# Decoder layer on one core: the MLP's sums kept times the mean square, products in another order, gate by halves of the tokens, last norm token-major

## Chip, cores and metric

One core of one Trainium2 chip runs one step of a decoder layer. The metric is the device time of that program in microseconds (us), the median of several runs.

## The reference, cut to what matters

```python
def rms_norm(x, gain):
    y = xf * lax.rsqrt(jnp.mean(xf * xf, axis=-1, keepdims=True) + EPS)
    return y * gain
...
    x = x + jnp.concatenate([o, sg], axis=-1) @ w_out
    x = x + jnp.square(jax.nn.relu(rms_norm(x, g_ff) @ w_up)) @ w_down
    x = x + (p @ w_ple) * jax.nn.sigmoid(rms_norm(x, g_ple) @ w_ple_gate)
...
y_prompt = rms_norm(hp, g_final)
```

x has 1024 prompt tokens and 8 sample tokens of width 1024, the MLP has width 4096, p has width 256; all is float32. The mixer ahead of these lines (a gated delta rule and a spatial gate) isn't touched. Call X1 the x after the mixer. The relu is squared, so the factor of its norm can be taken out of the product: the MLP's sum over the rows of w_down is divided by the mean square of X1 (plus EPS) for each token.

## The kernel before

Activations lie feature-major: 128 features on the partitions, tokens along the row. Tokens are split into halves N1 and N2 (nn = 0, 1) and each of these into two pieces t of 256 and 260 columns (the 8 sample tokens lie at the end of the second), features of the result into halves M1 and M2 (ab). Every matmul operand is split into a high and a low part of type fp32r (`form`, `split_raw`, `split_gain`), and each product is three matmuls.

The up stage and the down stage multiply 2 x 2 blocks by the seven-product scheme of Winograd (P1 to P7). The up stage (`up_stage`) writes the squared relu and its sums to DRAM (f_d). Beside it `up_rows` writes X1 to DRAM (x1_d), sums its squares on ScalarE and GpSimd, and writes the reciprocal of the mean square of each token to row_d. The down stage (`down`) runs four quarters j of the inner dimension; each has the seven products in the order of DSTEPS, each product four column groups p of 128, each group two pieces t of 12 matmuls. It reads the activations of a product (raw, one buffer), splits them (`split_raw`), makes the weights of the next products four groups ahead (`down_forms`, RING = 4; GpSimd adds blocks of w_down where the scheme wants sums), and VectorE or ScalarE adds the PSUM tile to that product's accumulator:

```python
if j == 0:
    S.copy(a, ps)
else:
    V.tensor_add(a, a, ps)
```

In the last quarter the accumulators are added to each other, `finish` multiplies the MLP's sum by rr (the broadcast reciprocal), adds old X1 read back from DRAM and sums its squares, and `gate_in` multiplies by g_ple and splits for the gate. Then the gate: `gate_units((0, 2))` does eight column groups for N1, `gate_units((1, 3))` for N2. `rows` makes 1/rms for all tokens, `row_put` and `row_get` send it over DRAM to a broadcast tile; gate results wait in four PSUM tiles until it is there. `p_in` transposes p. Each block is multiplied by rr, put through a sigmoid, multiplied by the embedding product (`emb`) and added to X. The last norm sums squares feature-major on ScalarE and GpSimd, and `y_out` transposes and scales.

TensorE's order is the order of the program text, in which `weave` steps side tasks (`spawn`) into the matmuls by a hand-written clock (ROW, FIN0, YT, PT). In the down stage SP's DMA queue is in program order too. The other queues are ordered by the scheduler by priority and expected times; `high_priority` marks evictions and weights.

## Time and profile before

| | us |
|---|---|
| median of 3 runs (lowest, highest) | 1451.28 (1448.44, 1456.3) |
| the profiled execution | 1451.69 |
| its span | 1450.0 |
| TensorE busy in the span | 1322.1 |
| VectorE, ScalarE, GpSimd busy | 892.5, 676.9, 709.6 |

A busy share is an average over stages. PE is TensorE, PEld its weight loads, DVE VectorE, ACT ScalarE, POOL GpSimd, SP the queue that issues the DMAs; L1382 is line 1382 of the kernel. The granted clock is the share of full speed (2.4 GHz) that TensorE had on average in a stretch; its two levels are 1.2 and 2.4 GHz.

### The profile page before, as it was taken

The numbers are of one execution on the slowest core, as the hardware profiler recorded it, in microseconds if no ns is written. First come the engines' busy times: TensorE is split into PE (matmuls) and PEld (weight loads), VectorE is DVE, ScalarE is ACT, GpSimd is POOL, SyncE is SP. The second block draws the span as 40 slices with busy tenths as digits, with TensorE's granted clock in tenths as the row PEclk, the third lists the DMA queues.
The fourth block names the chain that finished last, engine by engine and source line by source line (L and its number), as shares of the span: only waits on it lengthen the run. The fifth ranks groups of instructions, "written<-read, shape, count | busy, mean of one in ns | idle before, by whom it ended". The sixth has DMA issues, their size and how long they took to land.

```text
span 1450.0 us, 26432 instructions
## 1 busy us (share of the span) xinstructions
PE 1322.1 (91%) x10195; PEld 1292.2 (89%) x10195; DVE 892.5 (62%) x1719; ACT 676.9 (47%) x1427; POOL 709.6 (49%) x723
## 2 busy tenths in 40 slices
PE   6979978989999899799999999799999999538997
PEld 5979967989898899799999999799999999438997
DVE  7746655366937747554554444466777788984454
ACT  6665646422233226544554445465334333244553
POOL 5300988847416316666755565434232239763411
PEclk9999989999999999899999999999999999768999
DMA  7234525555437713245444553744352435121232
GB/s 245 81 90 136 153 66 163 154 159 151 125 84 208 221 56 126 79 150 161 133 141 131 160 162 111 275 163 174 107 187 90 176 125 180 47 71 47 86 105 74
DMA packets 209177, 193.99 MB, mean 134 GB/s; under 512 B 20928, under 2 KB 183947, under 8 KB 205460
## 3 DMA queue, kind: packets, MB, share of 16 engines
q1 hardware_dynamic: 209052, 192.31, 42.3%
q8 instruction: 80, 1.31, 0.4%
q14 instruction: 45, 0.37, 0.1%
HBM read 131.76 MB, written 60.62 MB: 133 GB/s over the span
## 4 chain that ended last, share of the span: by engine, by line
PE 68%; POOL 10%; DVE 10%; ACT 4%; DMA 3%; issue 3%; SPq 1%; DVEq 0%; POOLq 0%; ACTq 0%
PE A L1209 9%; PE D L1209 6%; PE d L1422 6%; PE d L1423 6%; PE d L1421 6%; PE g L209 5%; PE g L211 4%; PE g L210 4%; PE B L1209 3%; PE C L1209 3%; POOL xinv L644 3%; POOL it L643 3%; PE g L1613 2%; PE g L1615 2%; PE g L1614 2%
## 5 line engine op out<-in xcount | busy, mean ns | idle before, releaser
L1422 PE MATMUL d<-h,wlo 128*128 128x260 f32 (+1 forms) x896 | 258.9, 289 | 30.7 <-DVE wlo L153 30.7
L209 PE MATMUL g<-ra,whi 128*128 128x384 f32 (+3 forms) x800 | 274.4, 343 | 1.2 <-ACT ra L388 1.0
L1421 PE MATMUL d<-h,whi 128*128 128x260 f32 (+1 forms) x896 | 257.8, 288 | 5.9 <-ACT whi L150 5.9
L211 PE MATMUL g<-ra,whi 128*128 128x384 f32 (+3 forms) x800 | 257.6, 322 | 0.8 <-POOL ra L389 0.4
L1423 PE MATMUL d<-h,whi 128*128 128x260 f32 (+1 forms) x896 | 257.7, 288 | 0.0
L210 PE MATMUL g<-ra,wlo 128*128 128x384 f32 (+3 forms) x800 | 256.6, 321 | 0.0
L1422 PEld LDWEIGHTS d<-h,wlo 128*128 128x128 f32 x896 | 174.5, 195 | 33.1 <-DVE wlo L153 33.1
L1421 PEld LDWEIGHTS d<-h,whi 128*128 128x128 f32 x896 | 173.9, 194 | 6.5 <-ACT whi L150 6.5
L1423 PEld LDWEIGHTS d<-h,whi 128*128 128x128 f32 x896 | 174.2, 194 | 0.0
L209 PEld LDWEIGHTS g<-ra,whi 128*128 128x128 f32 x800 | 155.4, 194 | 3.4 <-ACT ra L388 1.4
L211 PEld LDWEIGHTS g<-ra,whi 128*128 128x128 f32 x800 | 155.0, 194 | 2.5 <-POOL ra L389 1.6
L210 PEld LDWEIGHTS g<-ra,wlo 128*128 128x128 f32 x800 | 155.8, 195 | 0.7 <-DVE wlo L153 0.3
L153 DVE TENSOR_TENSOR wlo<-st,whi 128x512 fp32r<-128x512 f32 x94 | 74.6, 794 | 46.5 <-ACT whi L150 45.1
L1339 DVE TENSOR_TENSOR h<-raw,h 128x1024 fp32r<-128x1024 f32 (+1 forms) x56 | 79.6, 1429 | 28.6 <-ACT h L1338 28.6
L153 DVE TENSOR_TENSOR wlo<-s,whi 128x512 fp32r<-128x512 f32 x64 | 50.5, 790 | 75.7 <-ACT whi L150 75.7
L1209 PE MATMUL A<-fb,whi 128*128 128x260 f32 (+1 forms) x512 | 97.0, 282 | 0.0
L643 POOL TENSOR_TENSOR it<-ainv,xinv 32x31 f32<-32x31 f32 (+15 forms) x124 | 75.0, 605 | 40.2 <-DMA ainv<-inv_d 30.8
L1236 ACT ACTIVATE q<-q 128x520 f32<-128x520 f32 (+1 forms) x128 | 78.4, 631 | 25.3 <-DVE q L1232 19.8
L644 POOL TENSOR_TENSOR xinv<-xinv,it 32x31 f32<-32x31 f32 (+15 forms) x124 | 80.9, 653 | 9.6
L150 ACT CAST whi<-st 128x512 fp32r<-128x512 f32 x96 | 58.9, 618 | 52.2 <-PE g L211 32.4
L1209 PEld LDWEIGHTS A<-fb,whi 128*128 128x128 f32 x512 | 80.9, 189 | 0.0
L1338 ACT CAST h<-raw 128x1024 fp32r<-128x1024 f32 (+1 forms) x56 | 58.8, 1057 | 33.5 <-PE d L1422 21.8
(441 smaller groups left out, 3550.1 us busy)
## 6 DMA issues: line engine op xcount, KB each, us to landing
raw<-f_d SPq DMA_DIRECT2D x28, 1032.0 KB
a<-in_w_down SPq DMA_DIRECT2D x16, 1024.0 KB
st<-in_w_in SPq DMA_DIRECT2D x24, 512.0 KB
ck<-ck_d SPq DMA_DIRECT2D x32, 320.0 KB
f_d<-tt SPq DMA_DIRECT2D x16, 520.0 KB
ra<-in_w_up SPq DMA_DIRECT2D x32, 256.0 KB
rb<-in_w_up SPq DMA_DIRECT2D x32, 256.0 KB
f_d<-tt SPq DMA_DIRECT2D x16, 512.0 KB
```

The costliest lines, as they stand in the source:

```text
L153: lo_eng.tensor_sub(dst_lo, src, f32(dst_hi))
L209: PE.matmul(ps[:, :w], lhsT=whi[k], rhs=xh, start=(k == 0), stop=False)
L210: PE.matmul(ps[:, :w], lhsT=wlo[k], rhs=xh, start=False, stop=False)
L211: PE.matmul(ps[:, :w], lhsT=whi[k], rhs=xl, start=False, stop=(k == nk - 1))
L643: G.tensor_mul(tv, a, x)
L644: G.tensor_sub(X[:, j + 1 :, :w], X[:, j + 1 :, :w], tv)
L1209: PE.matmul(ps, lhsT=a[:, k, :], rhs=x[:, c, k, :], start=(first and k == 0 and j == 0), stop=(k == 3 and j == 2), skip_group_check=True)
L1236: S.activation(v, v, func)
L1339: V.tensor_sub(lo[:, c], raw[:, c], f32(hi[:, c]))
L1421: PE.matmul(ps, lhsT=wh[:, k, :], rhs=xh[:, k, :], start=(k == 0), stop=False)
L1422: PE.matmul(ps, lhsT=wl[:, k, :], rhs=xh[:, k, :], start=False, stop=False)
L1423: PE.matmul(ps, lhsT=wh[:, k, :], rhs=xl[:, k, :], start=False, stop=(k == 3))
```

## The change

All sums of X1 are kept multiplied by the mean square of the token (mst). `up_rows` multiplies old X1 by it on GpSimd, takes N2's part from N1's for the features of M2, and writes that to x1_d. The down stage loads it into four accumulators before the first product, so that the products are added onto it; no accumulator is multiplied by rr or gets old X1 at the end. Norms that follow don't see a factor common to a token if EPS is multiplied by its square (ems); p is multiplied by mst instead. P1 is added to two accumulators (INTO), all evictions are VectorE's, and the order of the products is P1, P6, P7, P4, P2, P5, P3. N1's inputs of the gate are ready after P2; N2's are made inside the gate stage (`second_half`), with a mean square of its own. The last norm is token-major: `y_out` transposes a chunk of tokens, squares and sums it on ScalarE along the row, takes the root, and multiplies by it and g_final.

In the diff below "..." stands for what is left out; `placed` and `issue_after` set the place of an instruction in its queue behind a named one.

```diff
-DSTEPS = (("P1", 0), ("P5", 4), ("P6", 5), ("P7", 6), ("P4", 3), ("P2", 1), ("P3", 2))
+DSTEPS = (("P1", 0), ("P6", 5), ("P7", 6), ("P4", 3), ("P2", 1), ("P5", 4), ("P3", 2))
...
+    def tok_put(i, nn, tok):
+        ps = pss.tile([P, 512], F32, tag="B0" if pss is pu else "s2", name="msT")[:5, :P]
+        PE.transpose(ps, tok, ident)
+        row = tp.tile([5, P], F32, tag="row", bufs=1, name="row")
+        V.tensor_copy(row, ps)
+        SY.dma_start(row_d[i, nn], row)
+    def tok_get(i, nn, c, out):
+        SY.dma_start(out, row_d[i, nn].rearrange("a b -> (a b)")[c : c + out.shape[1]].partition_broadcast(P))
...
+        G.memset(mst, 1.0)
...
-        V.reciprocal(tok, tok)
-        yield ROW
-        row_put(tok, 1, pu.tile([P, 512], F32, tag="B0", name="msT")[:, :P])
+        V.tensor_mul(ems, mst, mst)
+        V.tensor_scalar_mul(ems, ems, EPS)
+        for nn in range(2):
+            yield ROW
+            tok_put(0, nn, mst[:, nn])
+        for t in range(2):
+            w = WT[t]
+            mb = tp.tile([P, 520], F32, tag=f"sq{t}", bufs=1, name="mb")[:, : 2 * w].rearrange("p (a b) -> p a b", a=2)
+            for nn in range(2):
+                tok_get(0, nn, TOFF[t], mb[:, nn])
+            for m in range(KD):
+                x = X1[m][:, 512 * t : 512 * t + 2 * w].rearrange("p (a b) -> p a b", a=2)
+                G.tensor_mul(x, x, mb)
+                if m >= 4:
+                    G.tensor_sub(x[:, 0], x[:, 0], x[:, 1])
+                SY.dma_start(x1_d[m, :, 512 * t : 512 * t + 2 * w].rearrange("p (a b) -> p a b", a=2), x)
+                yield 5.0
...
-    acc = {"P1": ACC[:, 0, 0], "P6": ACC[:, 0, 1], "P7": ACC[:, 1, 0], "P5": ACC[:, 1, 1]}
-    for name in ("P4", "P2", "P3"):
-        acc[name] = dac.tile([P, 4, 516], F32, name=f"acc_{name}")
+    C11, C12, P4, P7 = ACC[:, 0, 0], ACC[:, 0, 1], ACC[:, 1, 0], ACC[:, 1, 1]
+    P5, P3 = (dac.tile([P, 4, 516], F32, name=f"acc_p{i}") for i in (5, 3))
+    INTO = {"P1": (C12, C11), "P6": (C12,), "P7": (P7,), "P4": (P4,), "P2": (C11,), "P5": (P5,), "P3": (P3,)}
...
-    rr = xst.tile([P, 2, 516], F32, name="rr")
+    pt = xst.tile([P, NU, DPLE], F32, name="pt")
...
-            sums = dst.tile([P, 4, 4, P], F32, tag="s", name="sums")
+            s1 = dst.tile([P, 4, 4, P], F32, tag="s1", name="s1")
+            s2 = dst.tile([P, 4, 4, P], F32, tag="s2", name="s2")
             for name, _ in DSTEPS:
                 for p in range(4):
                     with tc.high_priority(PRI):
...
+                        if name == "P6":
+                            G.tensor_add(s1[:, p], a_of("A21", p), a_of("A22", p))
+                            G.tensor_sub(s2[:, p], s1[:, p], a_of("A11", p))
+                            f = s2[:, p]
+                        elif name == "P5":
+                            f = s1[:, p]
+                        elif name in ("P7", "P3"):
                             f = dst.tile([P, 4, P], F32, tag="t", name="sd")
...
-    def finish(ab, nn, p, xo):
+    def add_ss(ab, nn, p):
         a = ACC[:, ab, nn, p]
-        V.tensor_mul(a, a, rr[:, nn])
-        G.tensor_add(a, a, xo[:, p])
...
+        x1_old(C11, 0, 0)
         split_raw(0)
         load_raw(1)
         load_a(0, "A21")
         load_a(0, "A22")
+        x1_old(P7, 1, 1)
         load_a(0, "A12")
-        row_get(rr, 1)
+        x1_old(P4, 1, 0)
+        x1_old(P3, 0, 1)
+        SY.dma_start(pt, p_prompt[0, 0].rearrange("(c p) d -> p c d", p=P))
...
-                    to = {"P2": "P1", "P3": "P6"}.get(name, name) if end else name
-                    a = acc[to][:, p, TOFF[t] : TOFF[t] + w]
                     with tc.high_priority(PRI):
-                        if j == 0:
-                            S.copy(a, ps)
-                        else:
-                            V.tensor_add(a, a, ps)
+                        for to in INTO[name]:
+                            a = to[:, p, TOFF[t] : TOFF[t] + w]
+                            if j == 0 and (to is P5 or name == "P1" and to is C12):
+                                V.tensor_copy(a, ps)
+                            else:
+                                V.tensor_add(a, a, ps)
...
-                    if name == "P6":
-                        add(G, "P6", "P1")
-                        add(G, "P1", "P2")
-                    elif name == "P7":
-                        add(G, "P7", "P6")
-                        add(G, "P6", "P5")
-                        add(V, "P5", "P7")
-                        add(G, "P6", "P3")
+                        eng.tensor_add(x[:, p], x[:, p], y[:, p])
+                    if name == "P7":
+                        add(G, P7, C12)
                     elif name == "P4":
-                        add(V, "P7", "P4")
-                        finish(1, 1, p, xo[1, 1])
+                        add(V, P4, P7)
+                        gate_in(1, 0, p)
+                        add_ss(1, 0, p)
                     elif name == "P2":
-                        finish(1, 0, p, xo[1, 0])
-                        gate_in(1, 0, p)
-                    elif name == "P3":
-                        finish(0, 0, p, xo[0, 0])
                         gate_in(0, 0, p)
+                        add_ss(0, 0, p)
...
-            elif i == 3:
-                xo[1, 1] = x1_old("A11", 1, 1)
-                xo[1, 0] = x1_old("A21", 1, 0)
-            elif i == 4:
-                xo[0, 0] = x1_old("A22", 0, 0)
-            elif i == 5:
-                xo[0, 1] = x1_old("A11", 0, 1)
         for p in range(4):
-            finish(0, 1, p, xo[0, 1])
+            G.tensor_add(C12[:, p], C12[:, p], P5[:, p])
+            V.tensor_add(P7[:, p], P7[:, p], P5[:, p])
+            G.tensor_add(C12[:, p], C12[:, p], P3[:, p])
...
-    for p in range(4):
-        for ab in range(2):
-            gate_in(ab, 1, p)
...
+    pt8 = [ty.tile([TS // 2, DPLE], F32, name=f"pt8{nn}") for nn in range(2)]
+    for nn in range(2):
+        SY.dma_start(pt8[nn], p_sample[0, 4 * nn : 4 * nn + 4, 0, :])
+    SY.dma_start(gfb, g_final.partition_broadcast(P))
...
+        for nn in range(2):
+            for q0 in (0, 2, 4):
+                qs = (q0, q0 + 1) if q0 < 4 else (4,)
+                for q in qs:
+                    src = pt[:, q // 2 * 4 + 2 * nn + q % 2, :] if q < 4 else pt8[nn]
+                    G.tensor_scalar_mul(src, src, mst[: rows_of(q), nn, q : q + 1])
...
+            arrived("p", nn)
...
+    def rows(nn):
+        ps = pss.tile([P, 16], F32, tag="s2", name="ms")
+        tok = tp.tile([P, 5], F32, tag="tok", bufs=2, name="tok")
+        V.memset(tok, 1.0)
...
+            root(tok[:, :], "rp", False)
+        yield ROW
+        with tc.high_priority(2 * PRI):
+            tok_put(1, nn, tok)
+            tok_get(1, nn, 0, rr[:, nn])
+        arrived("r", nn)
+    def y_out(nn, q):
+        r = rows_of(q)
+        c = q // 2 * 4 + 2 * nn + q % 2
+        yo = ty.tile([P, D], F32, tag="yo", bufs=2, name="yo")
+        st = tp.tile([P, 2], F32, tag="st2", bufs=2, name="st2")
+        pa = []
+        for a in range(2):
+            ps = pss.tile([P, 512], F32, tag="s2", name="yT")
+            for j in range(4):
+                PE.transpose(ps[:r, j * P : j * P + P], ACC[:, a, nn, j, q * P : q * P + r], ident)
+            S.activation(yo[:r, :512], ps[:r], AF.Square, accum_out=st[:r, a : a + 1])
+            pa.append(ps)
+            yield YT
+        V.tensor_add(st[:r, 0:1], st[:r, 0:1], st[:r, 1:2])
+        V.scalar_tensor_tensor(st[:r, 0:1], in0=st[:r, 0:1], scalar=1.0 / D, in1=ems[:r, nn, q : q + 1], op0=ALU.mult, op1=ALU.add)
+        root(st[:r, 0:1], "ry", True)
+        y = y_prompt[0, c * P : (c + 1) * P, :] if q < 4 else y_sample[4 * nn : 4 * nn + 4, 0, :]
+        for a in range(2):
+            b = slice(512 * a, 512 * a + 512)
+            V.scalar_tensor_tensor(yo[:r, b], in0=pa[a][:r], scalar=st[:r, 0:1], in1=gfb[:r, b], op0=ALU.mult, op1=ALU.mult)
+            SY.dma_start(y[:, b], yo[:r, b])
...
-                (V if q7 else G).tensor_add(xv, xv, t)
-                if q7 and m == KD - 1:
-                    S.activation(q7[0][:, n // 2, :w], xv, AF.Square)
-                    V.tensor_scalar_mul(xv, xv, gfin[:, m : m + 1])
-                else:
-                    if m == 0:
-                        S.activation(blk(ss, n), xv, AF.Square)
-                    else:
-                        q = tp.tile([P, 260], F32, tag="q", name="q")[:, :w]
-                        S.activation(q, xv, AF.Square)
-                        G.tensor_add(blk(ss, n), blk(ss, n), q)
-                    S.activation(xv, xv, AF.Copy, scale=gfin[:, m : m + 1])
+                (V if last and m > 5 else G).tensor_add(xv, xv, t)
...
+    def second_half():
+        for p in range(4):
+            for ab in (1, 0):
+                gate_in(ab, 1, p)
+                add_ss(ab, 1, p)
+                yield 2.0
+        yield 4.0
+        yield from rows(1)
     def first_out():
-        tok = tok_stat(ss, first)
-        yield FIN
-        for c in first:
-            while c == first[-1] and not gated:
-                yield 0.5
-            yo = ty.tile([P, D], F32, tag="yo", bufs=2, name="yo")
-            for a in range(2):
-                y_out(c, a, yt(c, a, pss, "s2"), tok, yo)
-                yield YT
-    gated = []
+        for q in range(5):
+            yield from y_out(0, q)
...
+        spawn(rows(0))
+        spawn(p_in())
+        spawn(second_half(), 6.0)
+        weave(gate_units((0, 2), False))
         spawn(first_out(), FIN0)
+        weave(gate_units((1, 3), True))
         drain()
+        for q in range(5):
+            for _ in y_out(1, q):
+                pass
```

## Rows read from the trace of the kernel before

**Rows 1.** The page: the busy tenths of TensorE and the granted clock in 40 equal slices.

```profile
PE   6979978989999899799999999799999999538997
PEclk9999989999999999899999999999999999768999
```

**Rows 2.** Stretches of the span, us from its start: length, then busy time and number of instructions of PE, PEld, DVE, ACT and POOL, granted clock, DMA share and GB/s.

```profile
1000.00:1195.00 195.00, 195.00 (x1639) 195.00 (x1639) 151.23 (x234) 79.06 (x110) 59.73 (x40) 1.00 0.40 142
1195.00:1287.80 92.80, 65.58 (x453) 63.45 (x452) 86.65 (x96) 27.34 (x41) 77.14 (x48) 0.83 0.29 97
1287.80:1320.00 32.20, 12.47 (x70) 11.63 (x69) 17.48 (x39) 14.53 (x26) 15.74 (x10) 0.69 0.22 65
1320.00:1434.70 114.70, 114.70 (x964) 114.68 (x964) 57.24 (x132) 58.75 (x128) 32.75 (x42) 1.00 0.25 75
916.00:940.00 24.00, 14.61 (x100) 13.78 (x98) 11.16 (x10) 11.88 (x21) 12.41 (x10) 0.86 0.78 274
```

**Rows 3.** Who TensorE waited for from 1000 to 1320 us: us in total, times, the longest.

```profile
PE d L1422 <- DVE wlo L153: 26.9, 9, 8.1
PE pT L1540 <- DMA pt<-in_p_prompt: 15.5, 1, 15.5
PE ms L1129 <- POOL ss L1386: 4.2, 1, 4.2
```

**Rows 4.** Groups of instructions from 1195 to 1290 us, shapes kept apart: count, busy us, mean ns of one, then the idle time before them.

```profile
L1382 DVE TENSOR_TENSOR acc<-acc,rr 128x516 f32<-128x516 f32 x16 | 22.5, 1409 | 0.0
L1383 POOL TENSOR_TENSOR acc<-acc,a 128x516 f32<-128x516 f32 x15 | 23.7, 1577 | 8.8 <-DVE acc L1382 8.8
L1437 POOL TENSOR_TENSOR acc<-acc 128x516 f32<-128x516 f32 x12 | 21.1, 1764 | 10.3 <-DVE acc L1430 10.3
L1437 POOL TENSOR_TENSOR acc<-acc,acc_P 128x516 f32<-128x516 f32 x8 | 14.5, 1822 | 0.0
L167 DVE SCALAR_TENSOR_TENSOR xs<-acc,vec,xs 128x516 fp32r<-128x516 f32 x8 | 10.8, 1356 | 0.0
L153 DVE TENSOR_TENSOR wlo<-a,whi 128x512 fp32r<-128x512 f32 x8 | 11.0, 1388 | 0.0
L153 DVE TENSOR_TENSOR wlo<-sd,whi 128x512 fp32r<-128x512 f32 x8 | 7.9, 991 | 1.8 <-ACT whi L150 1.8
L1430 DVE TENSOR_TENSOR acc<-acc,d 128x256 f32<-128x256 f32 x15 | 6.2, 410 | 2.0 <-PE d L1423 2.0
L1339 DVE TENSOR_TENSOR h<-raw,h 128x1040 fp32r<-128x1040 f32 x3 | 5.6, 1854 | 0.0
```

**Rows 5.** The same view from 1000 to 1200 us.

```profile
L153 DVE TENSOR_TENSOR wlo<-a,whi 128x512 fp32r<-128x512 f32 x28 | 26.2, 938 | 3.1 <-ACT whi L150 3.0
L153 DVE TENSOR_TENSOR wlo<-sd,whi 128x512 fp32r<-128x512 f32 x19 | 16.0, 843 | 2.7 <-ACT whi L150 2.7
L1339 DVE TENSOR_TENSOR h<-raw,h 128x1040 fp32r<-128x1040 f32 x18 | 24.8, 1379 | 0.2 <-ACT h L1338 0.2
L1430 DVE TENSOR_TENSOR acc_P<-acc_P,d 128x256 f32<-128x256 f32 x24 | 10.0, 416 | 0.6
L1360 POOL TENSOR_TENSOR sums<-sums,a 128x512 f32<-128x512 f32 x12 | 15.6, 1298 | 38.5 <-DVE wlo L153 38.5
```

**Rows 6.** Instructions in order of time at the gate's start: start us, us, engine, line; in brackets the idle time before it and who ended it.

```profile
1315.63 0.36 DVE L1136 TENSOR_SCALAR tok<-ms 128x2 f32<-128x2 f32 x4 [2.16 <-PE ms L1129]
1328.98 0.42 DVE L1589 TENSOR_TENSOR t<-g,rr 128x256 f32<-128x256 f32 x1 [2.71 <-DMA rr<-row_d]
```

**Rows 7.** Up stage: two groups of GpSimd from 600 to 905 us, one stretch (columns as in rows 2), and the two stores of the statistics row, with first and last start.

```profile
L1267 POOL TENSOR_TENSOR ssu<-ssu,qu 128x520 f32<-128x520 f32 x7 | 10.2, 1455 | 1.4 <-ACT qu L1266 1.4
L1246 POOL TENSOR_TENSOR tt<-q,tt 128x256 f32<-128x256 f32 x15 | 17.3, 1156 | 0.2
700.00:800.00 100.00, 100.00 (x841) 99.93 (x840) 48.58 (x91) 50.53 (x96) 60.95 (x53) 1.00 0.45 141
L1153 SPq DMA_DIRECT2D row_d<-row x2: 298/309/320, 741.6 to 1322.5; - x2
```

**Rows 8.** Start of the down stage: SP's DMA queue in order of time, and the stretch with the highest DMA rate (columns as in rows 2).

```profile
925.08 0.45 SPq L1331 DMA_DIRECT2D raw<-f_d  x1
925.58 2.51 SPq L1346 DMA_DIRECT2D a<-in_w_down  x3
934.89 34.16 SPq L1331 DMA_DIRECT2D raw<-f_d  x4
930.00:940.00 10.00, 7.96 (x65) 7.54 (x63) 3.47 (x3) 5.25 (x10) 4.76 (x4) 1.00 1.04 382
```

**Rows 9.** The tail, in order of time, of TensorE, ScalarE, VectorE and SP's queue.

```profile
1434.65 2.78 PE L1571 MATMUL yT<-ident,acc 128*128 128x128 f32 x24
1436.41 1.28 ACT L261 ACT_TABLE_LOAD   x1
1439.65 0.21 ACT L261 ACTIVATE rpr<-tok 128x9 f32<-128x9 f32 x1 [1.95 <-DVE tok L1138]
1440.81 1.41 DVE L1580 TENSOR_SCALAR yo<-yT,tok 128x512 f32<-128x512 f32 x2
1441.52 5.75 SPq L1581 DMA_DIRECT2D out<-yo  x10
1444.36 0.69 ACT L1578 ACTIVATE yo<-yT,tok 128x512 f32<-128x512 f32 x1 [1.50 <-DMA out<-yo]
```

More of the change, by code (lines that the diff above doesn't have):

```diff
@@ L1115, in trunk_step_kernel @@
     psx.close()
-    def chunk(v, c):
-        return v[:, :, 512:516] if c == NU else v[:, c // 2 % 2, TOFF[c // 4] + c % 2 * P : TOFF[c // 4] + c % 2 * P + P]
-    def tok_sums(ps, ss, chunks, more=None):
-        for c in chunks:
-            r = P if c < NU else TS
-            v = chunk(ss, c)
-            if c == NU:
-                s8 = tp.tile([P, 2, 4], F32, tag="s8", bufs=1, name="s8")
-                V.tensor_copy(s8, v)
-                v = s8.rearrange("p a b -> p (a b)")
-            PE.matmul(ps[:r, c : c + 1], lhsT=v, rhs=ones[:, 0:1], start=True, stop=not more)
-            if more:
-                PE.matmul(ps[:r, c : c + 1], lhsT=more[c], rhs=ones[:, 0:1], start=False, stop=True)
@@ L1149, in row_put, with rows_of @@
[L1149 to L1160 removed]
+    def rows_of(q):
+        return P if q < 4 else TS // 2
@@ L1278, in up_rows @@
+            v = ss.rearrange("p (a b) -> p a b", a=2)
+            for nn in range(2):
+                for q in (2 * t, 2 * t + 1) + ((4,) if t else ()):
+                    c = q % 2 * P if q < 4 else 256
+                    r = rows_of(q)
+                    PE.matmul(ps[:r, 5 * nn + q : 5 * nn + q + 1], lhsT=v[:, nn, c : c + r], rhs=ones[:, 0:1], start=True, stop=True)
+            pv = ps[:, :10].rearrange("p (a b) -> p a b", a=2)
             with tc.high_priority(PRI):
-                tok_mean(tok, ps, range(4 * t, 4 * t + 4 + t))
+                V.tensor_scalar(mst[:, :, 2 * t : 2 * t + 2], pv[:, :, 2 * t : 2 * t + 2], 1.0 / D, EPS, op0=ALU.mult, op1=ALU.add)
+                if t:
+                    V.tensor_scalar(mst[: TS // 2, :, 4], pv[: TS // 2, :, 4], 1.0 / D, EPS, op0=ALU.mult, op1=ALU.add)
@@ L1584, in gate_units @@
+    def gate_units(blocks, last):
         for m in range(KD):
@@ L1635, in trunk_step_kernel, with arrived @@
-    first, second = (0, 1, 4, 5), (2, 3, 6, 7, NU)
-    def first_out():
-        tok = tok_stat(ss, first)
-        yield FIN
-        for c in first:
-            while c == first[-1] and not gated:
-                yield 0.5
-            yo = ty.tile([P, D], F32, tag="yo", bufs=2, name="yo")
-            for a in range(2):
-                y_out(c, a, yt(c, a, pss, "s2"), tok, yo)
-                yield YT
-    gated = []
+    held, there = [], set()
+    def arrived(what, nn):
+        there.add((what, nn))
+        if there >= {("p", nn), ("r", nn)}:
+            for n, ev in list(held):
+                if n % 2 == nn:
+                    held.remove((n, ev))
+                    ev()
@@ L1683 @@
+        drain()
+        for q in range(5):
+            for _ in y_out(1, q):
+                pass
 _INS = [
```

190 lines of the change are left out of this document (50 added, 140 removed).

## Prediction

> **What bounds the kernel now.** First the page: TensorE's row of busy tenths is at 9 through the second half and drops in one place only, to 5, 3 and 8 shortly before the end, where the granted clock drops too [rows 1]. So the question is what that hole is worth and who makes it. Second, the stretches [rows 2]. From 1000 to 1195 us TensorE never pauses: 195 us for 1639 matmuls, 0.119 us each, 11.4 us for one of the seven products (96 matmuls). I use this as the yardstick: the lost time of a stretch is its length less 0.119 us per matmul recorded there, which counts idle time and time at the lower clock together (0.83, 0.69 of full speed). End of the down stage, 1195 to 1287.8: 453 matmuls are 53.9 us, lost 38.9. Start of the gate, 1287.8 to 1320: 70 matmuls are 8.3 us, lost 23.9. Start of the down stage, 916 to 940: 100 matmuls are 11.9 us, lost 12.1. The gate from 1320 to 1434.7 loses nothing, and from there to 1450.0 remain 15.3 us of tail. Third, who is waited for [rows 3]: 26.9 us for the low halves of weights (wlo) that VectorE writes, 15.5 for the p tokens, 4.2 for the sum of squares. Fourth, what keeps VectorE there: it is busy 86.65 of the 92.8 us and GpSimd 77.14 [rows 2], and the groups [rows 4] name finish (the products with rr, and GpSimd's additions of old X1) and the additions between accumulators.
>
> **End of the down stage.** The change removes the 16 VectorE products with rr, 22.5 us, and from GpSimd the additions of old X1, 23.7 us recorded there [rows 4]. Of the additions between accumulators GpSimd did 20 (21.1 + 14.5 us); 12 stay, four of them for the very end. VectorE keeps 8, and the 8 gate_in products (10.8 us). So VectorE has at least 86.65 - 22.5 = 64.2 us if nothing becomes shorter: lost 64.2 - 53.9 = 10.3. But its operations were stretched there: wlo took 1.39 and 0.99 us [rows 4] against 0.94 and 0.84 in the calm stretch [rows 5], split_raw 1.85 against 1.38. GpSimd falls to about 77.1 - 23.7 - 8 x 1.8 = 39 us, so part of this stretching goes; with the calm durations for 19 wlo and 6 split_raw, and a like share off 16 additions and products (1.4 to about 1.0), VectorE falls by another 15 us, below TensorE's work. Bounds of the lost time: 1 us, and 20 us if the order of VectorE's queue keeps weights behind additions as now (half of today's loss). I take 10, near the first sum, because queue order survives. Gain 29 (19 to 38).
>
> **Start of the gate.** p_prompt is now loaded at the start of the down stage instead of after w_ple into the same two buffers, so the 15.5 us go; the gate's first half needs only the sums of token half 0, complete after P2, two products (23 us) before the end, so the 4.2 us and most of the low clock go. What is late next is rr: from the mean square (1315.63) to the first product with it (1328.98) passed 13.4 us [rows 6]. Four PSUM tiles of gate work cover 4 x 24 x 0.119 = 11.4 us of it, and the p transposes some 2 more. The first 10 scalings of p on GpSimd, up to 1.2 us each by the 256-wide row [rows 7], can run earlier, since p and mst are there; behind the last C12 additions they would cost up to 12. w_ple waits for P5's buffer and lands after the last product, about as late as rr. Lost 5 instead of 23.9, bounds 1 and 14: gain 19 (10 to 23).
>
> **Start of the down stage.** Added on SP's queue ahead of load_raw(2) are four loads of old X1 (eight transfers, 1 MB each load) and p (1 MB), less rr and the later x1_old loads. raw(1), A21 and A22 leave at 925.1 to 928.1 [rows 8]; behind them 5 MB more. At the highest rate of that stretch, 382 GB/s, the 8.3 MB from 925.1 on end at 946.8, and raw(2), issued at 934.89 today, lands at about 949.5; its split (1.4 us on VectorE after ScalarE's half) is ready at about 952, where the third product could start at about 951. The second product is now P6, with one more GpSimd sum ahead of its weights, at least 1.3 us [rows 5]. With a short fall of the clock: +5 (0 to 12). The queue also gets a new wait at its head: the first x1_old load waits for the last x1_d write, and behind it stand raw(1), A21, A22 and A12, for which TensorE waits; a write later than 925 would cost its delay one for one.
>
> **Accumulating.** Every product is now added on VectorE: P1 twice (32 evictions more) and 56 ScalarE copies of the first quarter moved there, 88 x 0.41 = 36 us of VectorE. Its load in the calm stretch is 151.23 of 195 us [rows 2], 8.9 us per product of 11.4; 8 more evictions in 7 products make 9.4. So TensorE hides it, at no price. Where the cover goes: P1 alone, 8.9 + 3.3 = 12.2 us, spilling 0.8 us into the next product, within the four forms prepared ahead. The evictions read PSUM and keep 0.41 us in the busy stretch as in the calm one [rows 4, 5].
>
> **Up stage.** up_rows adds on GpSimd 16 products of 520 columns and 8 subtractions of half that: 16 x 1.46 + 8 x 1.16 = 33 us [rows 7], spread over 80 us in which GpSimd is already busy 61% (49 us): 82 of 80, so these low-ranked products drift some us behind their places and the weight sums between them can, too. The statistics land at 741.6 today, so the last x1_d write comes at about 825, well before the 925 of its first reader. TensorE is at 100% there [rows 7]: +2 (0 to 12).
>
> **Gate.** Two ScalarE passes per block and a GpSimd sum go: hidden, since TensorE never pauses there [rows 2], so 0. New are five token chunks put out during its second half, each with Squares, a root on ScalarE and two buffers yo that come back only after the store. One chunk needs about 4.4 us (two Squares at the 0.69 of a copy of that width, 0.4 for two small sums, 1.2 from Sqrt to the end of the four small operations behind it, 1.4 for two products [rows 9]) and 2.8 us until its store has landed (issued 1441.52, next write at 1444.36); two buffers give 7.2 / 2 = 3.6 us a chunk, while the order written for TensorE brings one every 3.9 (two YT of 1.2, stretched by the embedding's matmuls, and 8 transposes at 0.11). So about even: +3 (0 to 20), the tables' changes included: Sqrt among Sigmoids makes up to 10 changes of 1.28 us [rows 9], on a ScalarE half busy.
>
> The Trainium skill (ScalarE: Activation LUTs, What ACT_TABLE_LOAD costs) counts 2.66 us for a change, a drain included, and asks to batch functions by set, which speaks against this part. The trace has 1.28 and no row for a drain. By the Trainium skill's figure the tail would be 1.4 us longer and the sum 1423.
>
> **Tail.** From the end of the last embedding matmul (1434.65): transposes 0.5, Squares 1.4, sums 0.4, change of tables 1.3, 1.2, products 1.4: first chunk written at 1440.9, landed at 1443.7; the third, in the same buffer, 4.4 + 2.8 later at 1450.9; the fifth at 1458.1, against 1450.0 now [rows 9]. Bounds +2 (buffers not binding) and +10: +8.
>
> **Sum.** -29 - 19 + 5 + 2 + 3 + 8 = -30. The profiled execution took 1451.69 us, 1.7 above its span and 0.4 above the median: 1451.7 - 30 = 1422.
>
> **Rivals.** (a) A new wait takes the place of p at the gate's start: scalings of p behind C12's additions, or w_ple behind P5's buffer. For it: GpSimd was the late one there; against: both can run earlier. The whole 19 us go: 1441. (b) The output of chunks binds the second half of the gate: each of five costs its whole chain of 4.4 + 2.8 + 1.3 less the 3.9 of its place, 4.6 x 5 = 23 instead of 3: 1442. (c) VectorE becomes the bound of the whole down stage. If P6's doubled sums keep GpSimd so busy that VectorE works at the durations of [rows 4] throughout, a product needs 64 x 0.41 / 7 = 3.8 for evictions, 2 x 1.85 for the split and 4 x 1.39 for the forms, together 13.1 us against 11.4: 1.7 x 28 = 48 us lost, in which the end's 10 are included: 1422 + 38 = 1460, and with the clock falling in the pauses about 1465, slower. It decides from about 12.5 us a product. Against it: 77% today and evictions that don't stretch. (d) Stretching goes with GpSimd's work, and the three new costs hide (-38 - 21 + 8): 1401.
>
> **Chances.** Forecast 0.55 (alone 1409 to 1434), (a) 0.17, (b) 0.08, (c) 0.10, (d) 0.10. The range goes from (d), 1400, to 1446, above (a) and (b). About 0.5% (7 us) can be told from no change: faster than 1444 takes the forecast, (d) and most of (a) and (b), 0.84; same 0.07; slower, (c), 0.09.
>
> **What would show it.** After: no hole in TensorE's tenths but a notch at the gate's start; wlo waits under 12 us after the third quarter; no wait for p; VectorE about 82% in the middle of the down stage; TensorE at 100% through the up stage; a tail above 20 us with stores as releasers. I am wrong if VectorE reaches 100% in P1 and P6, if old X1 or raw(2) holds TensorE by 10 us or more, or if transposes wait for PSUM tiles in the gate's second half.

## The result: slower by half a per cent, in other places than forecast

The changed kernel takes 1460.43 us in the median of 17 runs against 1451.28 for 17 of the kernel before: ratio 1.0055, 95% interval 1.0038 to 1.0073. The forecast was 1422. The profiled execution took 1462.3 us (span 1460.6; before 1451.69 and 1450.0).

The page after, TensorE's busy tenths and its granted clock, to be held against [rows 1]:

```profile
PE   6979977989998999899949999769999999959996
PEclk9999989999999999999979999989999999989997
```

The hole before the end (5, 3, 8) is down to one 5. But there is a new hole (4) in the middle of the up stage and a deeper one (7, 6) at the start of the down stage. The stretches of the changed kernel (columns as in [rows 2]):

```profile
937.10:1000.10 63.00, 41.46 (x287) 40.30 (x287) 37.31 (x54) 18.21 (x26) 33.54 (x27) 0.81 0.68 238
1000.10:1293.40 293.30, 290.76 (x2407) 289.08 (x2406) 239.71 (x391) 117.98 (x167) 106.78 (x69) 0.99 0.37 129
1293.40:1321.40 28.00, 13.56 (x98) 12.64 (x97) 21.96 (x43) 15.94 (x30) 15.71 (x12) 0.76 0.28 85
700.00:765.00 65.00, 45.00 (x339) 44.09 (x338) 33.16 (x38) 18.58 (x34) 47.99 (x44) 0.82 0.48 156
```

By the yardstick of the forecast (length less 0.119 us per matmul; the tail is taken at its whole length), with the stages cut at the last matmul of each in either trace:

| stretch | lost before | lost after | difference | forecast |
|---|---|---|---|---|
| up stage from 560 us | 15.1 | 35.2 | +20.1 | +2 |
| first 63 us of the down stage | 12.1 | 28.8 | +16.7 | +5 |
| rest of the down stage | 39.2 | 6.9 | -32.3 | -29 |
| first 28 us of the gate | 21.8 | 16.3 | -5.5 | -19 |
| rest of the gate | 2.1 | 4.1 | +2.0 | +3 |
| tail | 15.9 | 22.8 | +6.9 | +8 |

That adds up to +7.9; the spans differ by 10.6, so 2.7 us are left for what lies ahead of 560 us. Three lines came out as forecast and three did not. The first line hides two opposite parts. The first 140 us of its stretch, before and after (columns as in [rows 2]):

```profile
560.00:700.00 140.00, 129.32 (x1051) 128.15 (x1050) 76.15 (x127) 79.22 (x153) 94.37 (x90) 0.95 0.40 127
560.00:700.00 140.00, 134.11 (x1099) 132.91 (x1098) 80.28 (x127) 80.88 (x157) 102.68 (x97) 0.99 0.37 118
```

Up to 700 us the loss fell from 14.9 to 9.2 us, and from there to the end of the up stage it rose from 0.1 to 26.0. The forecast has no term for the gain. In the kernel before ScalarE starts four squares of X1 from 581.08 us on, ahead of the next casts of the up stage's operands (586.18), and TensorE waits 5.9 us for such casts; the changed kernel ties the squares behind the up stage's own work, the casts start at 583.64, and the longest wait is 1.8. No run tests this by itself. Who TensorE waits for after 560 us (columns as in [rows 3], whose 26.9, 15.5 and 4.2 us have gone or shrunk):

```profile
PE d L1416 <- ACT whi L150: 16.0, 3, 10.6
PE D L1184 <- DVE wlo L153: 14.6, 2, 13.6
PE msT L1124 <- DVE tok L254: 13.4, 2, 12.7
PE yT L1582 <- DVE yo L1592: 9.2, 6, 4.2
PE d L1417 <- DVE wlo L153: 7.8, 6, 3.1
PE D L1184 <- ACT whi L150: 6.0, 1, 6.0
```

The same trace in order of time (start, us, engine, line; idle time before and its end in brackets), three excerpts: the up stage, the start of the down stage, the gate's start.

```profile
726.10 16.80 POOL L1273 TENSOR_TENSOR x<-x,mb 128x512 f32<-128x512 f32 x13 [4.82 <-DMA mb<-row_d]
742.86 1.26 POOL L1154 TENSOR_TENSOR s<-rb,ra 128x512 f32<-128x512 f32 x1
744.08 3.75 POOL L1273 TENSOR_TENSOR x<-x,mb 128x520 f32<-128x520 f32 x3
744.15 0.62 ACT L150 CAST whi<-s 128x512 fp32r<-128x512 f32 x1 [7.74 <-POOL s L1154]
744.80 14.11 DVE L153 TENSOR_TENSOR wlo<-s,whi 128x512 fp32r<-128x512 f32 x1 [11.21 <-ACT whi L150]
...
756.95 1.41 POOL L1223 TENSOR_TENSOR tt<-q,tt 128x256 f32<-128x256 f32 x2
758.97 0.58 PE L1184 MATMUL D<-fa,wlo 128*128 128x256 f32 x1 [13.56 <-DVE wlo L153]
759.05 1.59 POOL L1160 TENSOR_TENSOR s<-rb,ra 128x512 f32<-128x512 f32 x1 [0.69 <-DVE wlo L153]
...
942.65 3.19 SPq L1227 DMA_DIRECT2D f_d<-tt  x2
948.48 0.91 SPq L1369 DMA_DIRECT2D acc<-x_d  x2
949.49 0.46 SPq L1325 DMA_DIRECT2D raw<-f_d  x1
961.91 4.91 POOL L1353 TENSOR_TENSOR s<-a,a 128x512 f32<-128x512 f32 x4 [1.42 <-DMA a<-in_w_down]
966.78 5.86 POOL L1354 TENSOR_TENSOR s<-s,a 128x512 f32<-128x512 f32 x4
967.74 16.36 SPq L1325 DMA_DIRECT2D raw<-f_d  x2
...
1299.01 0.21 DVE L1564 SCALAR_TENSOR_TENSOR tok<-ms,ems 128x4 f32<-128x4 f32 x2
1299.15 1.65 DVE L167 SCALAR_TENSOR_TENSOR xt<-acc,vec,xt 128x516 fp32r<-128x516 f32 x1
1302.20 1.23 DVE L252 SCALAR_TENSOR_TENSOR rpt<-rpi,tok 128x5 f32<-128x5 f32 x1
1303.35 1.41 DVE L167 SCALAR_TENSOR_TENSOR xt<-acc,vec,xt 128x516 fp32r<-128x516 f32 x2
1312.88 0.17 DVE L254 SCALAR_TENSOR_TENSOR tok<-rpt,rpi 128x5 f32<-128x5 f32 x1
1313.61 0.28 DVE L1126 COPY row<-msT 5x128 f32<-5x128 f32 x1 [0.56 <-PE msT L1124]
1318.11 0.42 DVE L1601 TENSOR_TENSOR t<-g,rr 128x256 f32<-128x256 f32 x1 [0.23 <-DMA rr<-row_d]
```

In each a queue that runs in order holds small urgent work behind large work that is not urgent. Up stage: GpSimd starts 13 products of X1 in a row, and the weight sum (L1154) that TensorE needs comes behind them. Start of the down stage: SP's queue puts the first load of old X1 ahead of the second raw block, and GpSimd does four additions before the first difference. Gate: the small operations of N1's root, most of them 0.2 us each, alternate on VectorE with N2's gate inputs, then with p's low halves and w_ple's splits, and last from 1299.0 to 1312.9. What follows tests each.

### The profile page after: what moved, and what is told of

Same layout as the page of the kernel before. It is cut to its first block, busy times and chain, and to the rows that moved or that the text cites. A ratio compares the mean times of both kernels' runs of the same rounds, so it can differ in the third digit from the quotient of the medians.

```text
span 1460.6 us, 26483 instructions
## 1 busy us (share of the span) xinstructions
PE 1324.1 (91%) x10183; PEld 1290.2 (88%) x10183; DVE 914.0 (63%) x1832; ACT 651.7 (45%) x1361; POOL 690.9 (47%) x720
## 4 chain that ended last, share of the span: by engine, by line
PE 38%; DVE 7%; POOL 3%; issue 2%; DMA 2%; ACT 1%; SPq 0%; DVEq 0%; POOLq 0%; ACTq 0%
PE d L1417 6%; PE d L1418 6%; PE d L1416 6%; PE A L1184 5%; PE D L1184 3%; DVE wlo L153 2%; PE B L1184 2%; PE g L1614 2%; PE g L1615 2%; PE g L1616 2%; PE C L1184 2%; POOL x L1273 1%; DVE h L1333 1%; DMA a<-in_w_down 1%; DVE yo L1592 0%
## 5 line engine op out<-in xcount | busy, mean ns | idle before, releaser
L1416 PEld LDWEIGHTS d<-h,whi 128*128 128x128 f32 x896 | 172.6, 193 | 16.8 <-ACT whi L150 16.7
L153 DVE TENSOR_TENSOR wlo<-s,whi 128x512 fp32r<-128x512 f32 x96 | 94.0, 980 | 94.9 <-ACT whi L150 94.5
L150 ACT CAST whi<-s 128x512 fp32r<-128x512 f32 x96 | 59.3, 618 | 105.1 <-PE D L1184 26.5
L643 POOL TENSOR_TENSOR it<-ainv,xinv 32x31 f32<-32x31 f32 (+15 forms) x124 | 74.9, 604 | 40.0 <-DMA ainv<-inv_d 30.6
L1425 DVE TENSOR_TENSOR acc<-acc,d 128x260 f32<-128x260 f32 (+1 forms) x184 | 72.4, 414 | 28.6 <-PE d L1418 25.9
```

Source lines behind the costliest of these rows:

```text
L150: S.copy(dst_hi, src)
L153: lo_eng.tensor_sub(dst_lo, src, f32(dst_hi))
L643: G.tensor_mul(tv, a, x)
L1416: PE.matmul(ps, lhsT=wh[:, k, :], rhs=xh[:, k, :], start=(k == 0), stop=False)
```

## Experiments

Ratios are to the kernel before; "against the changed kernel" is the difference of the two ratios (the other is 1.0055) times 1451 us. Differences of under some 5 us say little by themselves: in the profiled executions the first matmul of the up stage, ahead of which no edit changes anything, comes anywhere from 575.6 to 584.5 us, and the up stage with the block of products in it varies by 5 us (last section). There the losses of the stretches decide.

| kernel | median us | ratio [95%] | against the changed kernel, us |
|---|---|---|---|
| e1_spread | 1433.2 | 0.9862 [0.9839, 0.9885] | -28 |
| e2_stores_late | 1459.5 | 1.0051 [1.0032, 1.0070] | -1 |
| e3_late_loads | 1453.7 | 1.0010 [0.9991, 1.0029] | -7 |
| e4_late_loads_alt | 1443.7 | 0.9950 [0.9921, 0.9980] | -15 |
| e5_rows_first | 1460.4 | 1.0050 [1.0035, 1.0064] | -1 |
| e10_row_first | 1455.0 | 1.0033 [1.0011, 1.0054] | -3 |
| e6_tail | 1452.0 | 1.0007 [0.9989, 1.0025] | -7 |
| e8_act | 1457.0 | 1.0053 [1.0033, 1.0073] | 0 |
| e9_finish_back | 1481.6 | 1.0199 [1.0172, 1.0225] | +21 |
| e7_all | 1418.0 | 0.9753 [0.9734, 0.9772] | -44 |
| e11_all | 1418.2 | 0.9783 [0.9764, 0.9802] | -39 |
| e12_all | 1409.6 | 0.9718 [0.9692, 0.9745] | -49 |

**The up stage: GpSimd's queue or SP's.**

```diff
+                with tc.issue_after(placed["pool"]):
+                    G.tensor_mul(x, x, mb)
+                    if m >= 4:
+                        G.tensor_sub(x[:, 0], x[:, 0], x[:, 1])
```

> Edit: the changed kernel, with GpSimd's X1 products and differences (L1273, L1275) each tied behind the latest store of an up period (the placed instruction of GpSimd), so that they stand singly between the periods' own work instead of as one block of 17 us. In the changed kernel TensorE had 339 products in the 65 us from 700 to 765 (24.7 us short of 0.119 us each), against next to nothing lost there in the kernel before. Theory A (the block in GpSimd's in-order queue holds back the weight sums, these the roundings, these TensorE): the loss in the up stage falls from 35 us to between 10 and 14 us, the time from 1460 to 1435 to 1442 us, that is 0.99 to 0.994 of the kernel before. Rival B (the products' volume on GpSimd is what is too much, wherever they stand): the loss spreads but stays at 20 us or more, the time stays over 1452 us. Rival C (it is the stores of X1 in SP's queue that hold back the weight loads): this order also spreads the stores, so A and C are told apart by the next kernel, not by this one.

```diff
-                SY.dma_start(x1_d[m, :, 512 * t : 512 * t + 2 * w].rearrange("p (a b) -> p a b", a=2), x)
+                stores.append((x1_d[m, :, 512 * t : 512 * t + 2 * w].rearrange("p (a b) -> p a b", a=2), x))
                 yield 5.0
+        for dst, x in stores:
+            with tc.issue_after(placed["sp"]):
+                SY.dma_start(dst, x)
+            yield 2.5
```

> Edit: the changed kernel with the X1 products left as one block, but each of their stores issued on SP later, between the up periods, so that the up stage's weight loads no longer stand behind a row of eleven stores that took 18 us. Theory A (GpSimd's queue): the weight sums still stand behind the block, TensorE still goes nearly without work for over 15 us near 745 us, and the loss in the up stage stays at 28 us or more; time 1453 to 1463 us. Theory C (SP's queue): the loss falls to under 18 us and the time to 1435 to 1445 us. Between them (20 to 27 us) both queues hold a part.

With the same products spread, the up stage loses 12.6 us, less than the 15.1 before the change. The stretch of e1_spread:

```profile
700.00:765.00 65.00, 65.00 (x536) 64.94 (x536) 37.38 (x59) 31.70 (x60) 51.49 (x42) 0.98 0.55 176
```

TensorE never pauses, while GpSimd is busy 51.49 of the 65 us, more than in the changed kernel (47.99). From 700 us to the end of the up stage e1_spread loses 1.6 us, against 0.1 in the kernel before and 26.0 with the block; that it loses less in all (12.6) comes from the time ahead of 700 us (11.0 for 14.9). The same stretch of e2_stores_late, with the stores moved and the block left:

```profile
700.00:765.00 65.00, 52.05 (x379) 50.64 (x378) 23.14 (x44) 21.63 (x40) 49.99 (x45) 0.87 0.30 93
```

Its up stage loses 30.5 us, and those of the five kernels with block and stores as they were, and without the long operation of the last section, lose 30.4 to 31.9. So it is GpSimd's order (the time of e1_spread is even 2 us below the range of theory A); the volume of products costs some 1.5 us, and the stores nothing that can be told.

**The start of the down stage: two queues.**

```diff
-        x1_old(C11, 0, 0)
         split_raw(0)
         load_raw(1)
         load_a(0, "A21")
         load_a(0, "A22")
-        x1_old(P7, 1, 1)
-        load_a(0, "A12")
-        x1_old(P4, 1, 0)
-        x1_old(P3, 0, 1)
-        SY.dma_start(pt, p_prompt[0, 0].rearrange("(c p) d -> p c d", p=P))
+        x1_old(C11, 0, 0)
...
             load_raw(n + 2)
+            if n == 0:
+                x1_old(P7, 1, 1)
+            elif n == 1:
...
```

> Edit: the changed kernel with the loads of old X1 into the accumulators, and that of the prompt rows, moved on SP's queue behind the second load of raw f blocks and the first A21 and A22, one in each of the next periods. In the changed kernel the start of the down stage (first 63 us) lost 28.8 us against 12.1 before; the second raw load came 12.3 us after the end of the up stage, against 8.9. Theory A (SP's queue, held by the first accumulator load, delays raw and the weights): the loss falls to 16 to 22 us, time 1448 to 1455 us. Rival B (the weight sums on GpSimd, whose four additions come ahead of the first difference, end last): raw comes earlier, but the roundings of s2 begin where they did, the loss stays within 3 us of 28.8 and the time at 1457 to 1463 us.

In e4_late_loads_alt the sums alternate too:

```diff
+                            with tc.issue_after(placed["sum"]) if p else ExitStack():
+                                G.tensor_add(s1[:, p], a_of("A21", p), a_of("A22", p))
+                            placed["sum"] = G.tensor_sub(s2[:, p], s1[:, p], a_of("A11", p)).ins
```

> Edit: the kernel of the late accumulator loads, with the weight sums of the down stage in the order addition, difference, addition, difference on GpSimd instead of four additions and then four differences. Theory A (loads alone): no more than 2 us better than the kernel with the late loads alone. Theory B (the order of the sums): the first rounding of s2 begins some 4 us earlier, 4.91 us of additions being four of 1.23 us, so the loss at the start of the down stage falls by 4 to 8 us against the late loads alone. With both, the loss is 10 to 18 us and the time 1442 to 1450 us.

Lost in the first 63 us: 28.8 in the changed kernel, 24.0 with the late loads, 17.3 with both. SP's queue in e3_late_loads, then GpSimd in e4_late_loads_alt:

```profile
942.72 0.45 SPq L1325 DMA_DIRECT2D raw<-f_d  x1
952.92 0.33 SPq L1325 DMA_DIRECT2D raw<-f_d  x1
```

```profile
950.45 1.28 POOL L1354 TENSOR_TENSOR s<-a,a 128x512 f32<-128x512 f32 x1 [0.24 <-DMA a<-in_w_down]
951.81 1.27 POOL L1355 TENSOR_TENSOR s<-s,a 128x512 f32<-128x512 f32 x1
```

The up stage ends at 933.9 in the first of these traces, so raw(1) leaves 8.8 us after it instead of 12.4 (949.49 - 937.1), and raw(2) 19.0 instead of 30.6 (967.74 - 937.1). Behind raw(1) stand the blocks of w_down that GpSimd adds: its first addition starts 24.8 us after the up stage in the changed kernel (961.91) and 20.7 in e3_late_loads, as in the kernel before. The loads alone brought 4.8 us, less than the 7 to 13 expected: there the first difference still stood behind four additions. In the second trace it comes 1.4 us after the first addition. So each queue held a part, 4.8 and 6.7 us.

**The gate's start: three links of one chain.**

```diff
+                with tc.issue_after(placed["root"]):
+                    gate_in(ab, 1, p)
...
+                    with tc.issue_after(placed["root"]):
+                        V.tensor_sub(lo, ps[:, :w], f32(hi))
```

> Edit: the changed kernel with VectorE's gate inputs of N2 and low halves of p tied behind the last operation of the root of N1's mean square, so that the nine small dependent operations of that root stand together in VectorE's queue. In the changed kernel the root took 13.9 us on VectorE (1299.0 to 1312.9) against 3.1 before (1315.6 to 1318.7), and TensorE waited 12.7 us for it. Theory A (other operations between the small ones): the root takes 3 to 5 us, the first product with rr comes about 9 us sooner, the first 28 us of the gate lose 6 to 9 instead of 16.3, the time is 1450 to 1455 us. Rival B (the covers end there, and p, w_ple or N2's inputs are late next): the root is short but the stretch still loses 13 us or more, or the gate after it loses what was gained; time 1457 to 1464 us.

```profile
1298.05 1.02 DVE L248 TENSOR_SCALAR rpi<-tok 128x5 int32<-128x5 int32 x1
1300.91 0.17 DVE L254 SCALAR_TENSOR_TENSOR tok<-rpt,rpi 128x5 f32<-128x5 f32 x1
1300.99 5.78 DVE L167 SCALAR_TENSOR_TENSOR xt<-acc,vec,xt 128x516 fp32r<-128x516 f32 x7
1306.69 0.41 DVE L1529 TENSOR_TENSOR pp<-pT,pp 128x256 fp32r<-128x256 f32 x1
1307.16 0.38 PE L1125 MATMUL msT<-ident,tok 128*5 128x128 f32 x1 [7.88 <-DVE pp L1529]
1312.90 0.27 DVE L1127 COPY row<-msT 5x128 f32<-5x128 f32 x1
```

In these lines of e5_rows_first the root takes 3.0 us (1298.05 to 1301.08), yet the row is copied at 1312.90: p's transposes stand ahead of the root's on TensorE and wait for low halves of p, which now stand behind seven gate inputs. The first 28 us of the gate lose 14.7 us. The theory of the root alone fell; the rival held.

```diff
-        V.tensor_copy(row, ps)
+        placed["row"] = V.tensor_copy(row, ps).ins
...
+                with tc.issue_after(placed["row"]):
+                    gate_in(ab, 1, p)
```

> Edit: the changed kernel with VectorE's gate inputs of N2 tied behind the copy of N1's statistics row (L1126), so that neither the root nor the low halves of p nor that copy stands behind them. With the root alone first (root 2.9 us instead of 13.9), TensorE still reached the transposition of the root at 1307.2, because p's transposes stand ahead of it and their low halves on VectorE stood behind seven gate inputs of N2; the copy of the row followed at 1312.9, behind the splits of w_ple. Theory A (the whole chain root, low halves of p, copy of the row, and not the root alone, sets the gate's start through VectorE's queue): the row is copied some 6 to 9 us earlier, the first 28 us of the gate lose 7 to 11 us instead of 16.3, and the time is 1450 to 1455 us. Rival B (after the row the gate's start waits for something else, such as the splits of w_ple or p's products on GpSimd): the row is early, but the loss stays at 13 us or more, time 1457 to 1464 us.

```profile
1295.24 0.28 DVE L1127 COPY row<-msT 5x128 f32<-5x128 f32 x1 [0.47 <-PE msT L1125]
1301.69 0.27 PE L1524 MATMUL pT<-ident,pt 4*128 4x4 f32 x1 [6.49 <-POOL pt L1517]
1306.07 0.41 DVE L1602 TENSOR_TENSOR t<-g,rr 128x256 f32<-128x256 f32 x1
```

The row is copied 8.1 us after the down stage's last matmul (1295.24 against 1287.1) instead of 20.2 (1313.61 against 1293.4). The loss is 12.9 instead of 16.3: the row is earlier than expected (12 us for 6 to 9), the gain is less, just where the rival begins. Late next are the sample rows of p, for whose scaling on GpSimd TensorE waited 6.49 us, and, behind the gate inputs, the splits of w_ple; the first product with rr comes 19.0 us after the down stage.

**The tail.**

```diff
-        yo = ty.tile([P, D], F32, tag="yo", bufs=2, name="yo")
+        yo = ty.tile([P, D], F32, tag="yo", bufs=4, name="yo")
+        jk = ty.tile([P, 512], F32, tag="jk", bufs=1, name="jk")
...
-            S.activation(yo[:r, :512], ps[:r], AF.Square, accum_out=st[:r, a : a + 1])
+            S.activation(jk[:r], ps[:r], AF.Square, accum_out=st[:r, a : a + 1])
```

> Edit: the changed kernel with four output buffers yo instead of two, the Squares written to a tile of their own, and the second PSUM tile of N2's chunks taken from the gate's pool, so that neither a store nor a PSUM tile holds up the next chunk at the end. Theory A (buffers make the tail long): the tail of 22.8 us falls to 17 to 20 and the time to 1455 to 1458 us. Rival B (the chain of five chunks on ScalarE and VectorE is the tail, at 3.4 us a chunk with a change of tables in each): the tail stays within 1.5 us of 22.8 and the time over 1458 us.

The tail is 18.6 us instead of 22.8, as the theory of the buffers has it. The time fell by more, 7 us. In the profiled executions the rest lies ahead of the down stage, where this edit changes nothing: the first matmul of the up stage comes 3.7 us earlier, and the up stage is 4.8 us shorter (last section). That the medians differ for the same reason is likely and not shown.

**What the end of the down stage gained, and the evictions.** In e9_finish_back the two operations act on a row of zeros, for four accumulators of four blocks:

```diff
+    def finish(a):
+        a, z = a.rearrange("p (b c) -> p b c", b=2), zer[:, None, :].to_broadcast([P, 2, 258])
+        V.tensor_add(a, a, z)
+        G.tensor_add(a, a, z)
```

> Edit: the changed kernel with the work of the former finish put back at the same four places as neutral operations: for each of 16 accumulator blocks one VectorE and one GpSimd operation with two inputs of 516 columns that adds zeros. Theory A (the end of the down stage gained 32 us because this work is gone, VectorE and GpSimd having been the late ones there): the rest and end of the down stage, which lost 6.9 us against 39 in the kernel before, lose 22 to 40 us again, and the time is 1475 to 1495 us. Rival B (it gained because of the order of the products and of the sums, which leaves more between accumulators and gate): it loses under 12 us and the time is 1460 to 1468 us.

The rest of the down stage in e9_finish_back:

```profile
992.30:1309.20 316.90, 296.78 (x2410) 294.73 (x2410) 262.01 (x405) 118.94 (x167) 133.09 (x85) 0.96 0.34 119
```

It loses 30.1 us (316.9 less 2410 x 0.119) instead of 6.9: put back, this work alone costs 23.2 of the 32.3 us. Its places are those of the new order, with two of the four accumulators behind the last product, where the kernel before had one. The remaining 9 us are the fewer additions between accumulators and the order together, which were not taken apart.

```diff
-                                V.tensor_copy(a, ps)
+                                S.copy(a, ps)
```

> Edit: the changed kernel with the first quarter's copies out of PSUM (P5, and P1 into the second accumulator, 64 x 0.41 us = 26 us of VectorE) put back on ScalarE. Theory A (TensorE hides these evictions, as the forecast had it): the time stays within 3 us of 1460 us and the rest of the down stage loses 6 to 9 us as it does. Rival B (VectorE's added evictions are part of the loss at the start of the down stage, where weights wait for low halves): the loss there falls from 28.8 by 3 us or more and the time to under 1456 us.

The ratio is the same, the loss at the start 28.5 (28.8), in the rest 7.2 (6.9): TensorE hides these evictions on either engine. But the edit moves only 16 of them, 8 of P1 and 8 of P5, 6.7 us of VectorE, and not the 64 and 26 us of its expectation: the other first-quarter evictions are now additions. So it tests a small part of the added load.

**All together.** e7_all joins the edits of e1_spread, e4_late_loads_alt, e5_rows_first and e6_tail; e11_all has the tie of e10_row_first in place of that of e5_rows_first; e12_all goes on from there, with the loads of p's sample rows ahead of w_ple's and the gate inputs later still.

> Edit: the changed kernel with all of these: the X1 products spread, the accumulator loads late and the weight sums alternating, the root first, the tail's buffers. Theory A (the causes are separate and add up): the first two measured -27 and -17 us; with 8 for the root and 3 for the tail the time is 1405 us, 1400 to 1415, faster than both kernels. Rival B (gains hide one another, because what is late next at the start of the down stage is the transfers' rate): 1416 us or more.

> Edit: the kernel with all edits (1418 us) with this tie in place of the one behind the root. Theory A: the gain of the tie alone, 6 to 9 us, is kept: 1409 to 1413 us. Rival B (the gate's start is bound by something else there): 1415 to 1420 us.

The time of e7_all is in the rival's range, but not for the rival's reason: its up stage loses 12.2 us, the start of the down stage 17.4 and the tail 18.3, as in the kernels with one edit each; only the root's 8 us failed to come (15.7 lost). e11_all with the early row loses 15.7 too: the row is copied at 1263.13, but the first product with rr stands behind the gate inputs and w_ple in VectorE's queue until 1274.99.

```diff
-                with tc.issue_after(placed["row"]):
+                with tc.issue_after(placed["rr"]):
                     gate_in(ab, 1, p)
...
-                V.tensor_mul(t, ps, blk(rr, n))
+                placed["rr"] = V.tensor_mul(t, ps, blk(rr, n)).ins
...
-        spawn(second_half(), 6.0)
+        spawn(second_half(), 10.0)
```

> Edit: the kernel with all edits and the early row (1418 us) with VectorE's gate inputs of N2 put behind the products with rr, one after each, instead of behind the copy of the row, and the loads of the eight sample rows of p ahead of those of w_ple. In the former the row was copied 9.2 us after the last product of the down stage, but the first product with rr came only after 21.1 us, behind eight gate inputs and the two splits of w_ple (3.4 us), and TensorE waited 4.2 us for the sample rows' scaling on GpSimd. Theory A (N2's gate inputs ahead in VectorE's queue are what is late next): the first product with rr comes 15 to 17 us after the down stage, the first 28 us of the gate lose 9 to 12 us instead of 15.7, and the time is 1411 to 1415 us. Rival B (the way of the row over DRAM or w_ple's own load is late next): the loss stays at 14 us or more and the time at 1416 us or more.

```profile
1264.59 0.28 DVE L1127 COPY row<-msT 5x128 f32<-5x128 f32 x1 [0.37 <-PE msT L1125]
1266.21 1.86 DVE L1514 TENSOR_TENSOR wpl<-st,wpl 128x1024 fp32r<-128x1024 f32 x1 [0.34 <-ACT wpl L1513]
1269.92 0.42 DVE L1611 TENSOR_TENSOR t<-g,rr 128x256 f32<-128x256 f32 x1 [0.57 <-DMA rr<-row_d]
```

The down stage ends at 1255.4 here, so the first product with rr comes 14.5 us after it (24.7 in the changed kernel), and rr itself is last. The gate's first 28 us lose 7.9, a little less than theory A's 9 to 12. With a ratio of 0.9718 to the kernel before, e12_all is faster than both: the change together with these edits (the four output buffers among them) brings 2.8%, some 41 us.

## Why the prediction was wrong, step by step

**End of the down stage, right.** Forecast -29, measured -32.3; putting the work of finish back costs 23.2.

**Accumulating, gate, tail, right.** From 1000 to 1195 us VectorE is busy 149.77 us (151.23 before) and TensorE 194.86; in e12_all VectorE reaches 163.41, 84% for the 82% forecast, and TensorE 195.00. Rival (c) did not happen. The rest of the gate cost 2.0 for 3, the tail 6.9 for 8; e6_tail confirms the two buffers behind 4.2 of it, and the 2.7 left are near the forecast's lower bound of +2 without them. A change of tables takes 1.28 us in the tail too: the load starts at 1440.95 and the square root at 1442.24. For this change the Trainium skill (ScalarE: Activation LUTs, What ACT_TABLE_LOAD costs) has 2.66 us, a drain included; nothing shows of a drain here.

**Up stage, +2 for +20.1: the step that failed is "spread over 80 us".** The 33 us of work were about rightly sized (26 us as a block, 31 in e1_spread). But the yields in the text space TensorE's program; GpSimd's queue is ordered by the scheduler, and the products came as 13 in a row. From 700 us on, where the products stand, the loss rose by 25.9 us, and some 5 of these belong to one long VectorE operation that six of nine profiled executions don't have (last section). Where the spreading is enforced (e1_spread), it rises there by 1.5 us, near the +2 forecast; the whole line is then -2.5, below the forecast's bounds (0 to 12), because of the 4 us gained ahead of 700 us that the forecast didn't name. The upper bound of 12 assumed some drift between neighbours, not a block.

**Start of the down stage, +5 for +16.7: two queues were named and priced too low.** The forecast saw that the first load of old X1 stands at the head of SP's queue, and made its price depend on the writes of X1. In fact it waited for the last store of the up stage (2.6 us in the waits of SP's queue), and raw(1) left 3.6 us later than in e3_late_loads. On GpSimd the forecast counted one sum more, 1.3 us; it was four additions in a row, 4.91 us. With both put right the stretch loses 17.3 us, 5.2 more than before. That is the size of the term, and only in part its mechanism: TensorE waits 4.0 us for the weights of P6 instead of 2.0 at the second product before, and from 955 to 960 us its granted clock is 0.50; but of the five loads that the forecast had ahead of raw(2) four stand behind it in this kernel, so the price of these transfers was not tested.

**Gate's start, -19 for -5.5: the 13.4 us from the mean square to rr [rows 6] were carried over unchanged.** In the kernel before VectorE had little else to do there. The change itself put N2's gate inputs and w_ple's splits beside the root and p's low halves in that queue, and 13.4 became 19.1 (1299.01 to 1318.11). Rival (a), a new wait in place of p's, is the nearest, though the waits are others than it named and 5.5 of the 19 us came. With the chain mended e12_all loses 7.9 us, inside the forecast's bounds (1 to 14) and above its 5.

Of the sum of -30, the failed terms account for 18.1 + 11.7 + 13.5 = 43.3 us, and the others gave 5.4 us more than forecast: -30 + 43.3 - 5.4 = +7.9.

## What to carry to other kernels

Work added to an engine with time to spare is not free by its share of the stage: ask in which order the queue will hold it, and what urgent small operation stands behind the largest run of it. A latency read from a trace (here mean square to rr) holds for the neighbours of that trace; when the change moves other work onto the same engine at the same place, it must be sized again. When a chain of small operations is mended link by link, time it end to end: the first product with rr came 24.7 us after the down stage, 24.8 with the root mended, 19.0 with the row, 14.5 with the last link.

## What the runs showed of the hardware

One VectorE operation with two inputs, the low half of a weight of 128x512, which takes 0.69 us where nothing holds it, ran from 744.80 to 758.91, 14.11 us, while GpSimd ran one operation behind the other; it ended in GpSimd's first pause (0.69 us, put down to this very operation), and TensorE's next matmul waited 13.56 us for it. The page "SBUF — State Buffer" of the Trainium skill (SBUF: two separate sides) says that a VectorE operation with two inputs in SBUF and a GpSimd operation that reads SBUF need the same port pair, which the one that starts first holds for its whole instruction while the other is blocked. The row agrees, and shows that the wait can go on over many instructions of the other. The same operation at the same place took 1.12 us in e6_tail, where GpSimd's three products beside it took 4.24 us instead of 3.75:

```profile
740.43 4.24 POOL L1273 TENSOR_TENSOR x<-x,mb 128x520 f32<-128x520 f32 x3
741.15 1.12 DVE L153 TENSOR_TENSOR wlo<-s,whi 128x512 fp32r<-128x512 f32 x1 [11.12 <-ACT whi L150]
```

Of the nine profiled executions with the block of products, three have the long operation; the stretch from 700 to 765 us loses 23.1 to 24.7 us there, 19.3 to 20.1 in the other six. There is one profiled execution of each kernel, so whether this goes by the execution or by the kernel stays open, and so does the cause.
